# Two-layer hybrid attention encoder: DMA loads in a written order at the start of attention, and softmax reciprocals spread through DRAM

## The chip, the cores and the metric

One NeuronCore of a Trainium2 chip runs the whole kernel. The metric is the device time of one execution in microseconds (us); the time of a kernel is the median of its runs. TensorE multiplies matrices and transposes, VectorE, ScalarE and GpSimd work on elements, SyncE (SP) issues most of the DMA transfers. In the profile they are PE, DVE, ACT, POOL and SP; PEld is TensorE's loading of weights.

## The reference

A trunk of two layers on 1024 tokens of width 1024. Each layer normalises `x`, projects it once to 2656 columns, and runs three groups of attention heads side by side:

```python
def hybrid_layer(x, g_norm, w_in, ...):
    z = rms_norm(x, g_norm) @ w_in
    aq, ak, av, ag, bq, bk, bv, bg, cq, ckv, ckr, cg = split(z)
    # A: 6 heads of 64, 2 key heads, all 1024 keys
    oa = dense_gqa_blocks(rope(norm(aq)), rope(norm(ak)), av) * silu(ag)
    # B: 6 heads of 64, 2 key heads, keys within 128 positions, a sink logit per head
    ob = windowed_sink_gqa(rope(bq), rope(bk), bv, sink) * silu(bg)
    # C: 4 heads of 64 + 32 rotary, low-rank q and kv, all 1024 keys
    oc = mla_blocks(...) * silu(cg)
    return x + concat(oa, ob, oc) @ w_out
```

After the second layer a last RMSNorm follows. Every softmax divides by its row's sum: here the reciprocals of these sums are multiplied into the gate, and the gate into the output.

## The kernel before

Everything is float32 split into a high and a low part, so that a product of two matrices is two or three passes of TensorE (`mm3`, line 136). Per layer the stages are: norm and transposes of `x` with the value projection, the projections of groups A, B and C, the gate projection (`pg`), attention, and the output projection (`pw`). Queries, keys, values and gates go through DRAM tensors (`d_q`, `d_k`, `d_kn`, `d_vc`, `d_gate`), attention's outputs through `d_o`.

Attention is a list of units that `units` yields and `pipeline` works off. A unit is one head (A, C) or three heads (B) of one 128-query tile: scores on TensorE (`sa`, `sb`, `sc`), a maximum on VectorE (L684, L922), the exponential on ScalarE with its row sum (L694, L942), transposes of the probabilities on TensorE (`ppa`, `ppb`, `ppc`, L703), their split into `pth` and `ptl` by ScalarE, GpSimd and VectorE (L710 to L715), and products with the values (`poa`, `pob`, `poc`). `pipeline` puts the scores of one unit ahead of the transposes of the unit before, and pieces of older value products between them. The query tile `qt` runs from 0 to 7 with six units of A and two of B each; C's units (groups of three query tiles; two head pairs `hp` of 0 and 1) are strewn between them after the half tiles in `C_AT`, and what remains of C follows at the end. Within these priorities a scheduler places each engine's instructions, the DMA issues of SP included; an engine then works them off in order.

`Gqa(g, qt, m0)` is a query tile of A or B: it loads the queries by four DMAs (`qsta`, `qstb`, in `qstack`), and takes the output tile `o`; its `gate` loads the gate (`gta`, `gtb`). `KeysC` loads group C's keys (`k`, in six DMAs for the first pair) and its values (`vC`), `GroupC` its queries by five DMAs a tile (`qc`). At the start of attention come A's and B's keys and first queries, the sink and the mask, then C's keys and queries, then the gates, by the program's order.

`divided` (L749 to L767) turns sums into gate factors, once for each query tile of A and of B and once for each group of C: 22 times in a layer. A query's sum lies on its partition, and the gate has queries along its free axis, so the reciprocals have to be turned: VectorE takes them (`rc`, L755), GpSimd copies each to 64 columns (`rw`, 128x384, one buffer, L757), TensorE transposes the three 128x128 blocks (`pr`, L763), ScalarE copies them out (`rb`, L765), and GpSimd multiplies the gate by them (L767). Later GpSimd multiplies the output by the gate (L800, L1090), and SP stores it to `d_o`.

`dma` (L93) issues on SP; in attention all its DMAs stay behind the last load of weights (`queue_behind`). Names in the profile leave out buffer numbers.

Of the kernel before, what the change touches and what calls it, by code (L numbers as in the profile page):

```python
# [8 lines left out]
F32 = mybir.dt.float32  # L9
# [36 lines left out]
def kernel(  # L46
# [22 lines left out]
    P = 128  # L69
    S, D = x.shape[1], x.shape[2]  # L70
    DEPTH = norm_g.shape[0]
    NS = S // P
# [5 lines left out]
    small = ctx.enter_context(tc.tile_pool(name="small", bufs=4))  # L78
    dram = ctx.enter_context(tc.tile_pool(name="dram", bufs=1, space=DRAM))

    queue_behind = [None]
    last_pow = [None]

    def after(ins, first):

        tc.add_manual_dep(
            ins,
            first.name,
            mybir.DependencyInfo(mybir.DependencyClass.NoSync, mybir.DependencyReason.DATA),
            reason="order",  # L90
        )
        return ins

    def dma(dst, src, eng=None):

        a, b = (t.bitcast(F32) if t.dtype == F32R else t for t in (dst, src))
        ins = (eng or nc.sync).dma_start(a, b)  # L97
        if queue_behind[0] is not None and eng is None:
            after(ins.ins, queue_behind[0])
        return ins.ins  # L100

    pinned = [False]
# [13 lines left out]
    V, G, A, T = Engine(nc.vector), Engine(nc.gpsimd), Engine(nc.scalar), Engine(nc.tensor)  # L116

    ident = const.tile([P, P], F32, name="ident")
    dma(ident, c_ident)
    mhalf = const.tile([P, 8], F32, name="mhalf")  # L120
    nc.vector.memset(mhalf, -0.5)
# [104 lines left out]
    for l in range(DEPTH):  # L226
# [8 lines left out]
        d_kn = dram.tile([2, 2, P, S], F32R, name=f"d_kn{l}")  # L235
        d_k3 = dram.tile([2, 64, S], F32R, name=f"d_k3{l}")
        d_vc = dram.tile([P, NS, 4, P], F32R, name=f"d_vc{l}")
        d_o = dram.tile([P, 8, S], F32, name=f"d_o{l}")

        vp_ = ExitStack()  # L240
# [4 lines left out]
        with stage.ph as ph:  # L245
# [6 lines left out]
            def ps_t(name):  # L252
                return ps1.tile([P, 512], F32, tag="T", name=name)
# [24 lines left out]
            if l == 0:  # L278
# [6 lines left out]
                def load_x(st):  # L285
                    xts[st] = stage.px.tile([P, D], F32, tag="xt", name=f"xt{l}_{st}", bufs=XBUFS)
                    queue_behind[0] = dma(xts[st], x_src[st * P : (st + 1) * P, :])
# [61 lines left out]
            for i in range(2):  # L349
                gq = g_small[:, i * 64 : i * 64 + 64]  # L350
                ins = G.tensor_tensor(
                    out=tabs[:, :, 2 * i, :],
                    in0=rope_a[:, :, 0, :],
                    in1=gq.unsqueeze(1).to_broadcast([P, NS, 64]),
                    op=ALU.mult,
                )
                after(ins.ins, behind)
                gv = gq.rearrange("p (h a c) -> p h a c", h=2, a=2)
                for a in range(2):
                    for h in range(2):  # L360
                        o = h * 32 + a * 16
                        ins = G.tensor_tensor(
                            out=tabs[:, :, 2 * i + 1, o : o + 16],
                            in0=rope_a[:, :, 1, o : o + 16],
                            in1=gv[:, h, 1 - a, :].unsqueeze(1).to_broadcast([P, NS, 16]),
                            op=ALU.mult,
                        )
# [22 lines left out]
            for st in range(NS):  # L390
                nm = f"{l}_{st}"
# [42 lines left out]
            for st in range(NS):  # L434
                nm = f"{l}_{st}"
# [219 lines left out]
        with ExitStack() as ph:  # L655
            ps2 = wa_.enter_context(tc.tile_pool(name=f"ps2_{l}", bufs=2, space=PSUM, reuse_waits="tile"))
            at = ph.enter_context(tc.tile_pool(name=f"at{l}", bufs=2, reuse_waits="tile"))
# [4 lines left out]
            pk_ = ExitStack()  # L662
            pk = pk_.enter_context(tc.tile_pool(name=f"pk{l}", bufs=1, side="right", reuse_waits="tile"))
            pq = pk_.enter_context(tc.tile_pool(name=f"pq{l}", bufs=1, side="right", reuse_waits="tile"))
            tcnt, qcnt = [0], [0]

            def ps_s(name):
                return ps2.tile([P, 512], F32, tag="S", name=name, bufs=SBANKS)
# [79 lines left out]
                    dma(t[r0 : r0 + 64, :, par, :], d_q[g][qt, i, 64 * par : 64 * par + 64])  # L748
                return t  # L749

            def divided(gt, sums, n, nm):

                pr = ps_t(f"pr{nm}")
                rc = small.tile([P, 3, 2], F32, tag="rc", name=f"rc{nm}")
                V.reciprocal(rc[:, 0:n, :], sums)  # L755
                wide = at.tile([P, 384], F32, tag="rw", name=f"rw{nm}", bufs=1)
                G.tensor_copy(  # L757
                    wide[:, 0 : n * P].rearrange("p (m a d) -> p m a d", a=2, d=64),
                    rc[:, 0:n, :].unsqueeze(3).to_broadcast([P, n, 2, 64]),
                )  # L760
                for m in range(n):
                    ms = slice(m * P, (m + 1) * P)
                    T.transpose(pr[:, ms], wide[:, ms], ident)  # L763
                rb = at.tile([P, 384], F32, tag="rb", name=f"rb{nm}")
                A.copy(rb[:, 0 : n * P], pr[:, 0 : n * P])  # L765
                gv = gt.rearrange("p g s -> p (g s)") if len(gt.shape) == 3 else gt
                G.tensor_tensor(out=gv, in0=gv, in1=rb[:, 0 : n * P], op=ALU.mult)  # L767

            class Gqa:
# [25 lines left out]
                def divide(self):  # L795

                    divided(self.gt, self.sm.rearrange("p (m a) -> p m a", a=2), 3, self.nm)

                def finish(self):
                    G.tensor_tensor(out=self.o, in0=self.o, in1=self.gt, op=ALU.mult)  # L800
                    dma(d_o[:, self.m0 : self.m0 + 3, self.qt * P : (self.qt + 1) * P], self.o)

            def pipeline(units, spare):


# [45 lines left out]


            if True:
                ks, start = {}, {}
                for g, m0 in (("a", 0), ("b", 3)):
                    start[g] = Gqa(g, 0, m0)
# [200 lines left out]
            class GroupC:  # L1057
# [25 lines left out]
                    dma(self.gt[:, 0 : self.n], d_gate[:, 6 + self.hp, self.q0 * P : self.q1 * P])  # L1083

                def divide(self):
                    divided(self.gt[:, 0 : self.n], self.sm.rearrange("p a g -> p g a"), self.nq, self.nm)

                def finish(self):
                    gt, o = self.gt[:, 0 : self.n], self.o[:, 0 : self.n]
# [39 lines left out]
            def groups_c():  # L1129
                for hp in range(2):  # L1130
                    ks = KeysC(hp)
                    for q0 in range(0, NS, 3):
                        c = GroupC(ks, hp, q0)
                        if hp or q0:
                            c.gate()
                        else:

                            for it in (start["a"], start["b"], c):
                                it.gate()
                            yield None  # L1140
                        for par in range(2):
                            grp = {}
                            yield [UnitC(c, par, g, grp) for g in range(c.nq)]

            def units():

                cs = groups_c()
                next(cs)
                for qt in range(NS):
                    if qt == 0:  # L1150
                        a, b = start["a"], start["b"]
                    else:
                        a, b = Gqa("a", qt, 0), Gqa("b", qt, 3)
                        a.gate()
                        b.gate()
                    for kv in range(2):
                        grp = {}
                        for g in range(3):
                            yield UnitA(a, kv, g, grp)
                            if g == 1:  # L1160
                                yield UnitB(b, kv)
                        if 2 * qt + kv in C_AT:
                            yield from next(cs)
                first = True
                for us in cs:
                    for u in us:
                        yield u
                        if first:
                            yield ab_done
                            first = False  # L1170
# [8 lines left out]
        with ExitStack() as ph:  # L1179
# [10 lines left out]
            for st in range(NS):  # L1190
                nm = f"{l}_{st}"
# [111 lines left out]
```

## Time and profile before

| | before |
|---|---|
| median of 3 runs (lowest to highest) | 1340.75 us (1340.05 to 1341.09) |
| the profiled execution's own time | 1342.18 us |
| its span in the profile | 1340.4 us |
| mean granted clock of TensorE | 0.988 of full speed |
| TensorE busy | 1301.9 us, 97% |
| VectorE busy | 892.3 us, 67% |
| ScalarE busy | 720.2 us, 54% |
| GpSimd busy | 524.6 us, 39% |

The profile is one execution. Busy times are unions of an engine's instructions; matmuls are pipelined, so TensorE's busy time says that it had something in flight, not that it ran at its peak. Attention's first scores start at 278.7 us in layer 0 and at 937 in layer 1; its last value products start at 598 and 1258. The number in the brackets of a timeline's row is the idle time of the engine before that instruction and what ended it.

### The profile page before, as it was taken

What the parts mean: (1) busy time and instruction counts of PE and PEld (TensorE: products, weight loads), DVE (VectorE), ACT (ScalarE), POOL (GpSimd) and SP (SyncE); (2) the same over time, 40 slices, a digit from 0 to 9 for tenths busy, and PEclk for the clock granted to TensorE, in tenths of its full rate; (3) what the DMA queues carried; (4) which work ended last, traced back from release to release, by engine and by line L of the source; (5) the groups of instructions that cost most, each with busy time, mean ns of one, the idle gap of its engine ahead of it and who ended that gap; (6) DMA issues with size and microseconds to landing.
All of it is one profiled execution on the core that took longest, in us unless ns stands there. A gap on an engine that the chain in (4) does not pass through costs nothing.

```text
span 1340.4 us, 21695 instructions
## 1 busy us (share of the span) xinstructions
PE 1301.9 (97%) x7320; PEld 1139.5 (85%) x7320; DVE 892.3 (67%) x2246; ACT 720.2 (54%) x1547; POOL 524.6 (39%) x602
## 2 busy tenths in 40 slices
PE   7999999989999999999999999999799999999997
PEld 7888998868989899888898889887698999998786
DVE  6685662057888988875537766600789899998543
ACT  4232341166888889842313324311688899897332
POOL 4330121025666676752023111300366766667100
PEclk8999999998999999999999999999899999999999
DMA  7234469353222432257323344783622225113443
GB/s 252 87 124 148 135 202 261 122 132 89 68 61 60 111 90 58 74 179 235 131 78 121 122 132 161 242 196 103 154 68 64 59 69 139 46 45 126 165 146 112
DMA packets 176878, 166.46 MB, mean 124 GB/s; under 512 B 22528, under 2 KB 149376, under 8 KB 176768
## 3 DMA queue, kind: packets, MB, share of 16 engines
q1 hardware_dynamic: 158016, 140.43, 36.5%
q10 hardware_dynamic: 18752, 24.65, 5.3%
q8 instruction: 58, 0.95, 0.3%
q14 instruction: 52, 0.43, 0.1%
HBM read 107.35 MB, written 57.67 MB: 123 GB/s over the span
## 4 chain that ended last, share of the span: by engine, by line
PE 82%; DVE 6%; DMA 5%; ACT 2%; issue 2%; SPq 2%; POOL 1%; POOLq 0%; DVEq 0%; ACTq 0%
PE pg L136 13%; PE pw L136 12%; PE pzb L114 7%; PE pza L114 7%; PE poa L136 6%; PE sc L136 5%; PE ppa L703 4%; PE pzc L136 4%; PE sa L136 4%; PE pzv L136 4%; PE ppc L703 3%; PE poc L136 3%; PE pob L136 2%; PE sb L136 2%; SPq L97 2%
## 5 line engine op out<-in xcount | busy, mean ns | idle before, releaser
L684 DVE CUSTOM_DVE_ANT_0 pa<-sa,zero 128x512 f32<-128x512 f32 x96 | 65.5, 682 | 136.6 <-PE sa L136 134.8
L711 POOL TENSOR_SCALAR ptha<-pfa 128x512 fp32r<-128x512 f32 x96 | 59.4, 621 | 206.7 <-ACT pfa L710 202.3
L712 POOL TENSOR_TENSOR ptla<-pfa,ptha 128x512 fp32r<-128x512 f32 x96 | 123.6, 1290 | 6.1
L136 PE MATMUL sa<-ka,qsta 128*128 128x512 f32 x384 | 121.3, 417 | 0.8 <-ACT g L617 0.7
L694 ACT ACTIVATE pa<-pa,nmxa 128x1024 f32<-128x1024 f32 x96 | 111.2, 1160 | 14.0 <-DVE nmxa L684 13.9
L136 PE MATMUL sc<-k,qc 128*128 128x512 f32 x384 | 111.5, 410 | 0.9 <-DVE nmxc L684 0.9
L703 PE MATMUL ppa<-ident,pa 128*128 128x128 f32 x768 | 106.3, 273 | 0.7 <-DVE ptlb L715 0.5
L703 PEld LDWEIGHTS ppa<-ident,pa 128*128 128x128 f32 x768 | 90.9, 141 | 14.8 <-DVE ptla L715 1.2
L136 PE MATMUL pw<-woh,oh 128*128 128x512 f32 x256 | 99.4, 394 | 2.1 <-ACT oh L1001 1.1
L136 PE MATMUL pw<-wol,oh 128*128 128x512 f32 x256 | 100.6, 394 | 0.8 <-DVE wol L1021 0.6
L136 PE MATMUL pg<-hTh,wh 128*128 128x512 f32 x256 | 100.3, 392 | 0.0
L136 PE MATMUL pg<-hTh,wl 128*128 128x512 f32 x256 | 100.2, 391 | 0.0
L136 PE MATMUL pg<-hTl,wh 128*128 128x512 f32 x256 | 100.1, 391 | 0.0
L136 PE MATMUL pw<-woh,ol 128*128 128x512 f32 x256 | 99.1, 393 | 0.3 <-DVE ol L1002 0.3
L216 POOL TENSOR_SCALAR wh<-wst 128x512 fp32r<-128x512 f32 (+1 forms) x64 | 39.6, 638 | 148.3 <-PE pzb L114 79.4
L617 ACT ACTIVATE g<-pg 128x512 f32<-128x512 f32 x32 | 19.1, 598 | 137.5 <-PE pg L136 90.5
L136 PE MATMUL poa<-ptha,vAB 128*128 128x384 f32 x256 | 89.4, 349 | 1.0 <-DVE ob L793 1.0
L136 PE MATMUL poa<-ptla,vAB 128*128 128x384 f32 x256 | 88.2, 344 | 0.0
L694 ACT ACTIVATE pc<-pc,nmxc 128x1024 f32<-128x1024 f32 x64 | 74.0, 1157 | 10.2 <-DVE nmxc L684 9.7
L136 PEld LDWEIGHTS sc<-k,qc 128*128 128x128 f32 x384 | 66.6, 189 | 10.7 <-DVE nmxc L684 2.0
L712 POOL TENSOR_TENSOR ptlc<-pfc,pthc 128x512 fp32r<-128x512 f32 x56 | 74.0, 1327 | 1.5
L684 DVE CUSTOM_DVE_ANT_0 pa<-sa,zero,nmxa 128x512 f32<-128x512 f32 x96 | 71.1, 743 | 4.5 <-PE sa L136 1.8
(217 smaller groups left out, 3817.3 us busy)
## 6 DMA issues: line engine op xcount, KB each, us to landing
wst<-in_w_in_dram SPq DMA_DIRECT2D x20, 512.0 KB, 3.6
d_gate<-g ACTq DMA_DIRECT2D x32, 256.0 KB, 2.4
wost<-in_w_out_dram SPq DMA_DIRECT2D x32, 256.0 KB, 2.9
wst<-in_w_in_dram SPq DMA_DIRECT2D x16, 384.0 KB, 4.4
qsta<-d_qa SPq DMA_DIRECT2D x64, 96.0 KB, 2.6
qstb<-d_qb SPq DMA_DIRECT2D x64, 96.0 KB, 2.6
k<-d_kn SPq DMA_DIRECT2D x12, 512.0 KB, 6.8
qc<-d_qc SPq DMA_DIRECT2D x96, 64.0 KB, 2.2
```

Source lines behind the costliest of these rows:

```text
L97: ins = (eng or nc.sync).dma_start(a, b)
L114: return lambda *a, **k: tc.keep_in_program_order(f(*a, **k))
L136: T.matmul(ps, lhsT=a, rhs=b, start=first and i == 0, stop=last and i == len(parts) - 1)
L216: G.tensor_scalar(h, f, 1.0, 0.0, ALU.mult, ALU.add)
L617: A.activation(g, ps, AF.Silu)
L684: V.tensor_tensor_reduce(p[:, c * 512 : (c + 1) * 512], ps, zero[:, 0:1].to_broadcast([P, 512]), -1.0, nmx[0][:, 0:1] if c else 3.0e38, AL ...
L694: A.activation(p, p, AF.Exp, scale=-1.0, bias=nmx[1][:, 0:1], accum_out=sm)
L703: T.transpose(pt[:, (j - q0) * P : (j - q0 + 1) * P], p[:, j * P : (j + 1) * P], ident)
L711: G.tensor_scalar(hi, f, 1.0, 0.0, ALU.mult, ALU.add)
L712: G.tensor_tensor(out=lo, in0=f, in1=hi.bitcast(F32), op=ALU.subtract)
```

## The change

It has three parts. `divided` gets a second way, used for all groups but the last two of C's second head pair (`near`): the reciprocals are transposed as they are (128x6 to 6x128, L776), ScalarE copies the six rows (`rt`, L778), SP stores them to a DRAM tensor `d_r`, and two DMAs load them back into `rb`, each spreading three rows over 64 partitions. `in_order` makes the DMAs of SP keep the program's order from the start of attention until the first group of C is made. And `units` makes the objects of query tile `qt + 1` (their query loads) in the middle of tile `qt`, and the gates of the first tile of A and B ahead of C's keys.

```diff
         if queue_behind[0] is not None and eng is None:
             after(ins.ins, queue_behind[0])
+        if in_order[0] and eng is None:
+            tc.keep_in_program_order(ins)
...
+        d_r = dram.tile([4 * NS, 6, P], F32, name=f"d_r{l}")
...
-            def divided(gt, sums, n, nm):
+            def divided(gt, sums, n, nm, near=False):
...
+                if near:
...
+                else:
+                    rc = rc.rearrange("p a m -> p (a m)")[:, 0 : 2 * n]
+                    V.reciprocal(rc.rearrange("p (a m) -> p m a", a=2), sums)
+                    T.transpose(pr[0 : 2 * n, 0:P], rc, ident)
+                    rt = at.tile([16, P], F32, tag="rt", name=f"rt{nm}")
+                    A.copy(rt[0 : 2 * n, :], pr[0 : 2 * n, 0:P])
+                    dr = d_r[rcnt[0], 0 : 2 * n]
+                    rcnt[0] += 1
+                    dma(dr, rt[0 : 2 * n, :])
+                    drv = dr.rearrange("(a m) s -> a (m s)", a=2)
+                    for a in range(2):
+                        dma(rb[64 * a : 64 * a + 64, 0 : n * P], drv[a].partition_broadcast(64))
                 gv = gt.rearrange("p g s -> p (g s)") if len(gt.shape) == 3 else gt
                 G.tensor_tensor(out=gv, in0=gv, in1=rb[:, 0 : n * P], op=ALU.mult)
...
             if True:
+                in_order[0] = True
...
-                    divided(self.gt[:, 0 : self.n], self.sm.rearrange("p a g -> p g a"), self.nq, self.nm)
+                    divided(self.gt[:, 0 : self.n], self.sm.rearrange("p a g -> p g a"), self.nq, self.nm, self.hp and self.q0)
...
-                            for it in (start["a"], start["b"], c):
-                                it.gate()
+                            c.gate()
                             yield None
...
+                a, b = start["a"], start["b"]
+                ahead = Gqa("a", 1, 0), Gqa("b", 1, 3)
+                a.gate()
+                b.gate()
                 cs = groups_c()
                 next(cs)
+                in_order[0] = False
                 for qt in range(NS):
-                    if qt == 0:
-                        a, b = start["a"], start["b"]
-                    else:
-                        a, b = Gqa("a", qt, 0), Gqa("b", qt, 3)
+                    if qt:
+                        a, b = ahead
                         a.gate()
                         b.gate()
                     for kv in range(2):
+                        if kv and 0 < qt < NS - 1:
+                            ahead = Gqa("a", qt + 1, 0), Gqa("b", qt + 1, 3)
```

How it moves instructions. SP at the start of attention in layer 0, before (`qstb_1` are the queries of B's second tile, `k_0` parts of C's keys, `qc_0_0` C's first queries):

```order
L97 DMA vC_0_2815<-d_vc_85 128x8x256
L97 DMA gta_0_2844<-d_gate_77 128x3x128
L97 DMA gtb_0_2846<-d_gate_77 128x3x128
L97 DMA gtc_0_0_2848<-d_gate_77 128x384
L97 DMA qsta_1_3133<-d_qa_78 64x3x128 x4
L97 DMA qstb_1_3140<-d_qb_79 64x3x128
L97 DMA k_0_0_2814<-d_kn_83 64x2x1024 x2
...
L97 DMA qc_0_0_2824<-d_qc_80 64x2x128 x2
...
L97 DMA qstb_1_3140<-d_qb_79 64x3x128 x3
L97 DMA gta_1_3147<-d_gate_77 128x3x128
```

and with the change:

```order
L98 DMA qsta_1_2815<-d_qa_78 64x3x128 x4
L98 DMA qstb_1_2822<-d_qb_79 64x3x128 x4
L98 DMA gta_0_2829<-d_gate_77 128x3x128
L98 DMA gtb_0_2831<-d_gate_77 128x3x128
L98 DMA k_0_0_2833<-d_kn_83 64x2x1024 x2
...
L98 DMA vC_0_2834<-d_vc_85 128x8x256
L98 DMA qc_0_0_2843<-d_qc_80 64x2x128 x2
...
L98 DMA gtc_0_0_2863<-d_gate_77 128x384
L98 DMA gta_1_3148<-d_gate_77 128x3x128
```

The four `qstb_1` stand together ahead of the keys; the two gates and `vC_0` now stand ahead of `qc_0_0`.

TensorE at the same place, before (`sb_1`: scores of B's second tile; `sa_1`: A's; `prb`: B's divisor transposes; `poa`: value products):

```order
L136 MATMUL sb_1_0_0_3240<-kb_0_2802,qstb_1_3140 128x384
L703 MATMUL ppb_0_1_2_0_3117<-ident,scb_0_1_3038 128x128 x2
L136 MATMUL sb_1_0_1_3244<-kb_0_2802,qstb_1_3140 128x384
L136 MATMUL sb_1_0_2_3248<-kb_0_2802,qstb_1_3140 128x384
L136 MATMUL sa_1_0_2_0_3287<-ka_0_2789,qsta_1_3133 128x512
L763 MATMUL prb_0_3122<-ident,rwb_0_3125 128x128 x3
L136 MATMUL poa_0_0_2_3025<-ptha_0_0_0_0_2874,vAB_90 128x384
```

and with the change (`sc_0_0_0`: the first scores of C):

```order
L139 MATMUL sb_1_0_2_3249<-kb_0_2803,qstb_1_2822 128x384
L139 MATMUL sa_1_0_2_0_3288<-ka_0_2790,qsta_1_2815 128x512
L139 MATMUL sa_1_0_2_1_3292<-ka_0_2790,qsta_1_2815 128x512
L707 MATMUL ppb_0_1_1_0_3121<-ident,scb_0_1_3053 128x128 x2
L139 MATMUL sc_0_0_0_0_0_3332<-k_0_0_2833,qc_0_0_2843 128x512
L139 MATMUL poa_0_0_2_3040<-ptha_0_0_0_0_2889,vAB_91 128x384
```

The first `sc` has moved ahead of the sixteen `poa`.

GpSimd at the divisions of the third query tile, before:

```order
L757 COPY rwb_2_4108<-rcb_2_4106 128x384
L757 COPY rwa_2_4176<-rca_2_4174 128x384
L767 TENSOR_TENSOR gtb_2_3762<-gtb_2_3762,rbb_2_4113 128x384
L711 TENSOR_SCALAR ptha_2_1_0_1_3993<-pfa_2_1_2_4_4167 128x4x128
L767 TENSOR_TENSOR gta_2_3760<-gta_2_3760,rba_2_4181 128x384
L712 TENSOR_TENSOR ptla_2_1_0_1_3995<-pfa_2_1_2_4_4167,ptha_2_1_0_1_3993 128x4x128
```

and with the change:

```order
L715 TENSOR_SCALAR ptha_2_1_0_1_4008<-pfa_2_1_2_4_4182 128x4x128
L716 TENSOR_TENSOR ptla_2_1_0_1_4010<-pfa_2_1_2_4_4182,ptha_2_1_0_1_4008 128x4x128
L786 TENSOR_TENSOR gtb_2_3763<-gtb_2_3763,rbb_2_4121 128x384
L715 TENSOR_SCALAR pthc_0_3_0_0_1_4222<-pfc_0_3_0_0_4_4240 128x4x128
L716 TENSOR_TENSOR ptlc_0_3_0_0_1_4224<-pfc_0_3_0_0_4_4240,pthc_0_3_0_0_1_4222 128x4x128
L786 TENSOR_TENSOR gta_2_3761<-gta_2_3761,rba_2_4189 128x384
```

The copies `rw` are gone, and both multiplications stand behind one split (`pth`, `ptl`) more.

SP with the change at the first divisions, where the new DMAs stand among query loads and output stores:

```order
L98 DMA qc_0_3_4131<-d_qc_80 64x2x128
L98 DMA d_r_86<-rtb_0_3142 6x128
L98 DMA d_r_86<-rta_0_3196 6x128
L98 DMA rbb_0_3138<-d_r_86 64x384 x2
L98 DMA rba_0_3192<-d_r_86 64x384 x2
L98 DMA d_o_87<-ob_0_2802 128x3x128
L98 DMA gta_2_3761<-d_gate_77 128x3x128
```

The stores to `d_r` and the loads of `rb` stand in front of the first store to `d_o` and of the gates of the third tile.

## Rows read from the trace of the kernel before

**Rows 1.** The page's part 1 (busy us, share, instructions) and part 4 (the chain).
```profile
PE 1301.9 (97%) x7320; PEld 1139.5 (85%) x7320; DVE 892.3 (67%) x2246; ACT 720.2 (54%) x1547; POOL 524.6 (39%) x602
...
PE 82%; DVE 6%; DMA 5%; ACT 2%; issue 2%; SPq 2%; POOL 1%; POOLq 0%; DVEq 0%; ACTq 0%
```

**Rows 2.** Stretches: length, busy PE, PEld, DVE, ACT, POOL; clock, DMA share, GB/s.
```profile
278.00:282.00 4.00, 3.75 (x16) 2.37 (x14) 2.69 (x9) 2.48 (x3) 0.00 (x0) 1.00 0.59 170
282.00:286.00 4.00, 3.91 (x26) 3.46 (x27) 3.57 (x17) 3.81 (x11) 0.79 (x2) 1.00 0.73 177
286.00:290.00 4.00, 3.83 (x22) 2.66 (x21) 3.86 (x15) 4.00 (x11) 2.25 (x3) 1.00 1.02 213
...
302.00:306.00 4.00, 2.31 (x7) 1.88 (x8) 1.52 (x5) 0.00 (x0) 0.00 (x0) 0.50 0.66 188
...
340.00:560.00 220.00, 217.29 (x1379) 196.87 (x1378) 193.01 (x534) 190.27 (x410) 149.45 (x167) 1.00 0.26 69
```

**Rows 3.** TensorE's timeline, layer 0: start, length, instruction, idle before and its releaser.
```profile
296.50 0.44 PE L703 MATMUL ppb<-ident,scb 128*128 128x128 f32 x2 [0.35 <-ACT pfa L710]
303.45 0.98 PE L136 MATMUL sb<-kb,qstb 128*128 128x384 f32 x2 [6.50 <-DMA qstb<-d_qb]
...
305.09 1.62 PE L136 MATMUL sb<-kb,qstb 128*128 128x384 f32 x4 [0.24 <-DMA qstb<-d_qb]
```

**Rows 4.** TensorE's timeline at the same place of layer 1.
```profile
960.64 0.98 PE L136 MATMUL sb<-kb,qstb 128*128 128x384 f32 x2 [5.62 <-DMA qstb<-d_qb]
...
962.51 1.65 PE L136 MATMUL sb<-kb,qstb 128*128 128x384 f32 x4 [0.46 <-DMA qstb<-d_qb]
```

**Rows 5.** SP's timeline at the start of attention, layer 0.
```profile
277.48 2.48 SPq L97 DMA_DIRECT2D qsta<-d_qa  x4
280.02 0.65 SPq L97 DMA_DIRECT2D qstb<-d_qb  x1
281.90 2.19 SPq L97 DMA_DIRECT2D k<-d_kn  x3
284.15 1.87 SPq L97 DMA_DIRECT2D k<-d_k  x3
286.06 14.86 SPq L97 DMA_DIRECT2D qc<-d_qc  x15
300.97 1.82 SPq L97 DMA_DIRECT2D qstb<-d_qb  x3
```

**Rows 6.** The chain that ended last, in order of time: start, length, what.
```profile
285.42 10.77 DMA k<-d_k
...
302.19 2.77 DMA qstb<-d_qb
...
313.99 0.33 PE pra L763 x3
```

**Rows 7.** Groups by line and form: busy us, mean ns of one, idle before, releasers.
```profile
L763 PE MATMUL pra<-ident,rwa 128*128 128x128 f32 x48 | 9.6, 272 | 0.0
...
L757 POOL COPY rwa<-rca 128x384 f32<-128x384 f32 x16 | 8.1, 505 | 56.2 <-PE prb L763 35.1 <-DVE nmxa L684 12.5 <-issue 5.9
...
L765 ACT COPY rba<-pra 128x384 f32<-128x384 f32 x16 | 7.9, 491 | 0.4 <-PE pra L763 0.4
...
L939 ACT ACTIVATE besb<-besb 128x3 f32<-128x3 f32 x32 | 6.2, 193 | 0.0
```

**Rows 8.** DMA issues: size of one, median us from issue to landing.
```profile
qsta<-d_qa SPq DMA_DIRECT2D x64, 96.0 KB, 2.6
...
vC<-d_vc SPq DMA_DIRECT2D x4, 1024.0 KB, 6.7
...
gta<-d_gate SPq DMA_DIRECT2D x16, 192.0 KB, 2.8
...
d_o<-ob SPq DMA_DIRECT2D x16, 192.0 KB, 2.1
```

**Rows 9.** Waits of SP over the whole run: total us, times, longest.
```profile
SPq L97 <- POOL ob L800: 134.0, 16, 19.0
```

More of the change, by code (lines that the diff above doesn't have):

```diff
@@ L81 @@
     queue_behind = [None]
+    in_order = [False]
     last_pow = [None]
@@ L664 @@
             pq = pk_.enter_context(tc.tile_pool(name=f"pq{l}", bufs=1, side="right", reuse_waits="tile"))
-            tcnt, qcnt = [0], [0]
+            tcnt, qcnt, rcnt = [0], [0], [0]
             def ps_s(name):
@@ L749, in qstack @@
                 return t
-            def divided(gt, sums, n, nm):
+            def divided(gt, sums, n, nm, near=False):
                 pr = ps_t(f"pr{nm}")
[L754 to L763, printed above, removed]
-                rb = at.tile([P, 384], F32, tag="rb", name=f"rb{nm}")
-                A.copy(rb[:, 0 : n * P], pr[:, 0 : n * P])
+                rb = at.tile([P, 384], F32, tag="rb", name=f"rb{nm}")
+                rc = small.tile([P, 2, 3], F32, tag="rc", name=f"rc{nm}")
+                if near:
+                    rc = rc.rearrange("p a m -> p (a m)").rearrange("p (m a) -> p m a", a=2)[:, 0:n, :]
+                    V.reciprocal(rc, sums)
+                    wide = at.tile([P, 384], F32, tag="rw", name=f"rw{nm}", bufs=1)
+                    G.tensor_copy(
+                        wide[:, 0 : n * P].rearrange("p (m a d) -> p m a d", a=2, d=64),
+                        rc.unsqueeze(3).to_broadcast([P, n, 2, 64]),
+                    )
+                    for m in range(n):
+                        ms = slice(m * P, (m + 1) * P)
+                        T.transpose(pr[:, ms], wide[:, ms], ident)
+                    A.copy(rb[:, 0 : n * P], pr[:, 0 : n * P])
+                else:
[10 more added lines that the diff above has]
+                        dma(rb[64 * a : 64 * a + 64, 0 : n * P], drv[a].partition_broadcast(64))
```

## The prediction

> **What bounds the kernel now.** I began with the page's table of busy time and its chain of waits: TensorE is busy 97% of the span, and 82% of the chain that ended last lies on it, against 6% on VectorE and 5% on transfers [rows 1]. Then I cut the span into stretches. In the steady part of layer 0's attention, 340 to 560 us, TensorE is busy 217.29 of 220 us at a granted clock of 1.00, VectorE 193.01, ScalarE 190.27, GpSimd 149.45 [rows 2]. So there a microsecond taken off TensorE should mostly be a microsecond off the time, while GpSimd has a third of its time free.
>
> The other place is the start of attention. TensorE's timeline shows it idle for 6.50 us, from 296.94 to 303.45, before the first scores of group B's second query tile (`sb`), and 0.24 us more before the next pair; the releaser is the load of `qstb` [rows 3]. Layer 1 shows the same, 5.62 and 0.46 us [rows 4]. [...] SP's timeline tells why the load is late: one of the tile's four pieces is issued at 280.02, then six loads of `k` and fifteen of `qc`, which take SP to 300.97, and only then the other three [rows 5]. The chain agrees: a `k` load, then SP's issues, then `qstb<-d_qb` 2.77 us [rows 6]. At 286 to 290 us the DMA engines are full, share 1.02 at 213 GB/s [rows 2].
>
> **Part 1: the transposes.** Forty of the 44 divisions (20 of 22 in each layer) replace their three transposes by one of 6x128 (the two-tile groups: two by one of 4x128). That removes 40 x 3 - 2 = 118 and adds 40: 78 fewer. One transpose lasts 272 ns [rows 7], but they are pipelined: three in a row take 0.33 us on the chain [rows 6], 0.11 us each. 78 x 0.11 = **8.5 us**. The bounds are 0 (TensorE would have waited for something else) and 78 x 0.272 = 21 us; I take the pipelined price because the steady stretch has few gaps to fill.
>
> **Part 2: copies.** GpSimd loses 40 wide copies of 0.505 us, ScalarE's copy of 128x384 at 491 ns becomes one of 6x128, nearest to the small activation of 193 ns [rows 7]: 20 us off GpSimd, 40 x 0.3 = 12 us off ScalarE. I cost both at **nothing**: TensorE's work covers them. If that cover were gone in part they would be a gain, 3 us at most by ScalarE's share of the chain (2% [rows 1], 12 of its 720 us); I keep that inside the range.
>
> **Part 3: the detour through DRAM.** Each of these divisions now goes reciprocal, transpose, ScalarE copy, a 3 KB store to `d_r`, two broadcast loads of 96 KB into `rb`, GpSimd's multiplication. The nearest transfers are `d_o<-ob` at 2.1 us and `qsta` at 2.6 us [rows 8], and SP spends about 0.6 us on an issue (2.48 us for four [rows 5]): 2.1 + 2.6 + 2 x 0.6 = 5.9 us, against 0.505 + 0.33 + 0.491 = 1.3 us for copy, transposes and copy before. So `rb` comes an estimated 4.6 us later. It is wanted by the multiplication of the gate, then by that of the output, then by the store; none feeds TensorE before the output projection. But two queues are held. SP waits in place for the ScalarE copy and for the store's landing, with query loads, gates and `d_o` stores behind it; SP already sits 134.0 us waiting for `ob` products [rows 9], and the query loads are issued one query tile ahead, so I take their delay as covered. GpSimd waits in place for `rb`, with the splits of the transposed probabilities (`pth`, `ptl`) behind it, which TensorE's value products need. The order puts the multiplication some instructions later than the old copy, behind a split or two, which hides most of the 5.9 us. I take **+2.5 us** for all of this; the bounds are 0 and 40 x 4.6 = 184 us, were each late `rb` to reach TensorE in full; 2.5 is close to the lower end because GpSimd is busy only 149.45 of 220 us [rows 2]. Also inside it: the next layer's norm weights are now loaded behind the first output rows, which is near its use.
>
> [...]
>
> **Part 4: the start of attention.** The four `qstb_1` loads now stand together, ahead of `k`, so that wait goes [rows 3, 4]. What it cost: 6.50 + 0.24 us idle, and the half-rate stretch from 303.45 to about 308, half of 4.6, 2.3 us: 9.0 us in layer 0, some 8 in layer 1. What is late next: the first scores of group C (`sc`), which TensorE's order now puts ahead of the 16 value products of `poa` and which need `k` and `qc_0_0`. In front of `qc_0_0` the pinned queue has newly put `vC_0` (1024 KB), two gates (2 x 192 KB) and three pieces of `qstb` (3 x 96 KB) [rows 8]: 1696 KB, or 1.74 MB. At 213 GB/s that is 8.2 us; before the full stretch the engines have idle share 0.41 and 0.27 in the two windows from 278 to 286 [rows 2], 4 x 0.68 = 2.7 us, which takes up part of it. So `qc_0_0` lands about 5.5 us later than now. Now it is no earlier than the `k` piece in front of it, which is done at 285.42 + 10.77 = 296.2 [rows 6]: about 302. TensorE, with no wait for `qstb`, runs 2.5 to 3 us of scores and transposes past 296.94 and stands at `sc` by about 299.7. That is a new stall of 2.5 to 4.5 us and some 1.5 us of lower clock: 5 us in place of 9. I take **4 us per layer, 8 in all**; the bounds are 0 (the whole wait only changes its name) and 17 (no stall is left). Moving `vC_0` itself costs nothing where it is used, some 35 us later.
>
> Making the next query tile's objects half a tile earlier moves only loads that are early already: **0**.
>
> **Sum.** -8.5 + 0 + 2.5 - 8 = -14.0 us against the profiled execution's 1342.18 us: 1328.2. The median of the runs, 1340.75, lies 1.43 below that execution, so **1327 us** on the scale of the medians.
>
> **The rivals.** Two of the changes in 1000 are about what a measurement of this kernel can tell from none: 2.7 us.
> - *GpSimd becomes the bound (slower).* Each late `rb` stops GpSimd, the splits behind it come late, and TensorE waits for them in `poa`, `poc`, `pob`. For it: the splits are in-order work on the same engine. Against it: GpSimd's third of free time, and the multiplication's later place. Parts 1 and 4 give 16.5 us; with 2.7 us on top, it takes 19.2 / 40 = 0.48 us per division reaching TensorE before the time is slower. At 0.7 us: 1340.75 - 16.5 + 28 = 1352. Chance 0.09.
> - *The start's wait only changes its name.* `vC_0` and the gates push `qc_0_0` to 305 or later, and TensorE idles as long as before at `sc`. For it: the full DMA engines. Part 4 is then 0: 1335. Chance 0.16.
> - *No new stall at the start.* `qc_0_0` lands by 300, or the scheduler's other work covers it; part 4 is 17: about 1317 to 1318. Chance 0.14.
> - *The transposes were hidden.* TensorE isn't what limits the steady stretch; VectorE and ScalarE are busy 88% and 86% of it [rows 2], so their chain may be, and part 1 gives nothing: about 1335. Chance 0.12. [...]
> - *Both gains fail*, or the losses of part 3 eat them: within 2.7 us of now. Chance 0.10.
>
> **How the numbers follow.** The forecast has the remaining 0.39. The range takes in the second to fourth rivals and the unknown 0 to 10 us of part 3: 1315 to 1338, which leaves out the rival that is slower and most of the last, 0.2 at most. Faster: 0.39 + 0.16 + 0.14 + 0.12 = 0.81; same 0.10; slower 0.09.
>
> **What would show it.** Right: 78 fewer transposes for `pr`; no idle time at `sb` for `qstb`; a gap of some 3 us before the first `sc`, released by a `qc` or `k` load; the steady stretches of both layers some 4 us shorter each, with TensorE's busy share unchanged; GpSimd's multiplication released now and then by a load of `rb`, with no matching idle time on TensorE. Wrong: idle time on TensorE at `poa` or `poc` released by `pth` or `ptl` of GpSimd; a gap at `sc` as long as the old one; a steady stretch that keeps its length though the transposes are gone; query loads that come late because SP stood at `d_r`.

## The result, and the profile after

The changed kernel takes **1383.78 us** (median of 4 runs, 1383.21 to 1384.62) against 1340.42 for the kernel before: a ratio of 1.0323, 95% interval 1.0305 to 1.0341. It is 3.2% slower. 1327 was forecast, in a range of 1315 to 1338; the chance given to "slower" was 0.09.

The page of the kernel after, its parts 1 and 4, to set against [rows 1]:

```profile
PE 1304.0 (94%) x7242; PEld 1130.2 (82%) x7242; DVE 886.5 (64%) x2246; ACT 711.6 (51%) x1547; POOL 504.9 (37%) x562
...
PE 71%; DMA 11%; DVE 6%; ACT 4%; issue 3%; POOL 3%; SPq 2%; POOLq 0%; DVEq 0%; ACTq 0%
```

78 transposes are gone (7320 to 7242 matmuls), yet TensorE's busy time has not shrunk, its share of the chain has fallen from 82 to 71%, and that of transfers has risen from 5 to 11%. So the kernel waits for transfers where it did not before. TensorE's timeline at the start of attention says where, layer 0 and then layer 1 (start, length, instruction, idle time before it and its releaser):

```profile
282.15 2.78 PE L139 MATMUL sa<-ka,qsta 128*128 128x512 f32 x5 [4.02 <-DMA ka<-d_ka]
292.16 0.98 PE L139 MATMUL sb<-kb,qstb 128*128 128x256 f32 x3 [7.22 <-DMA kb<-d_kb]
...
320.17 1.62 PE L139 MATMUL sc<-k,qc 128*128 128x512 f32 x3 [6.67 <-DMA qc<-d_qc]
...
967.47 2.55 PE L139 MATMUL sa<-ka,qsta 128*128 128x512 f32 x5 [3.03 <-DMA ka<-d_ka]
...
977.60 0.98 PE L139 MATMUL sb<-kb,qstb 128*128 128x256 f32 x3 [7.58 <-DMA kb<-d_kb]
...
1005.33 1.62 PE L139 MATMUL sc<-k,qc 128*128 128x512 f32 x3 [6.69 <-DMA qc<-d_qc]
```

The wait for `qstb_1` of [rows 3, 4] is gone, as forecast. In its place stand three, 17.9 us of idle time in layer 0 and 17.3 in layer 1. The third, at `sc`, was forecast (2.5 to 4.5 us) and is longer, 6.67 and 6.69; the other two are for loads that the prediction did not look at: the keys of A and B (`ka`, `kb`), which in the kernel before were there long ahead. SP's timeline shows their issue, first before, then after:

```profile
208.51 3.76 SPq L97 DMA_DIRECT2D qsta<-d_qa  x4
212.48 2.54 SPq L97 DMA_DIRECT2D ka<-d_ka  x4
215.06 2.67 SPq L97 DMA_DIRECT2D qstb<-d_qb  x4
219.73 6.16 SPq L97 DMA_DIRECT2D kb<-d_kb  x4
```

```profile
206.70 0.34 SPq L98 DMA_DIRECT2D d_qc<-qklc  x1
236.66 22.21 SPq L98 DMA_DIRECT2D qsta<-d_qa  x4
263.84 12.08 SPq L98 DMA_DIRECT2D ka<-d_ka  x4
275.96 8.62 SPq L98 DMA_DIRECT2D qstb<-d_qb  x4
284.68 2.56 SPq L98 DMA_DIRECT2D kb<-d_kb  x4
...
299.79 1.89 SPq L98 DMA_DIRECT2D k<-d_kn  x3
...
304.47 19.36 SPq L98 DMA_DIRECT2D qc<-d_qc  x15
```

The same sixteen loads in the same order, but they begin 28 us later, are spread over 50 us, and push everything behind them: `k` is issued at 299.79 (281.90 before [rows 5]). What SP waits for is in the list of waits (total us, times, longest), before and after:

```profile
SPq L97 <- DMA d_gate<-g: 68.9, 8, 14.6
```

```profile
SPq L98 <- DMA d_gate<-g: 140.3, 16, 29.6
```

The wait has doubled. In layer 0, eight of the waits now end at loads of `qsta`, `ka` and `qstb`, which read no gate. The windows show what that does to the bandwidth: in the gate projection's stretch the kernel after moves 126 GB/s (180 before), and soon behind it the engines are full (columns as in [rows 2]):

```profile
186.00:279.00 93.00, 92.13 (x418) 76.02 (x416) 15.16 (x38) 16.64 (x29) 7.42 (x13) 1.00 0.39 126
279.00:292.00 13.00, 2.78 (x5) 1.33 (x5) 2.74 (x8) 3.13 (x5) 0.00 (x0) 0.60 0.80 183
292.00:306.00 14.00, 11.64 (x63) 9.51 (x63) 9.11 (x33) 7.64 (x20) 3.96 (x5) 0.88 1.07 220
...
340.00:560.00 220.00, 210.49 (x1302) 186.10 (x1301) 186.63 (x515) 180.59 (x393) 142.14 (x151) 0.99 0.31 87
```

The granted clock falls with the waits: 0.60 and 0.88 in the second and third row. In the trace TensorE's granted clock is 0.50 from 281.6 to 295.3 and from 315.8 to 326.0 us, 23.9 us in this start; in the kernel before it is 10.2 us (298.3 to 308.6).

The last of these rows answers to the steady stretch of [rows 2]: TensorE is busy 210.49 us of 220 there, not 217.29, so a second, smaller loss lies in the steady part.

**A wait that no order of instructions shows.** In the traces each DMA of SP or ScalarE bears the number of a semaphore that its landing raises. There are eight of these numbers, 106 DMAs on each before (848 in all) and 121 after (968), in turn over both queues; they are the counters that the experiments speak of. In the kernel before, 840 DMAs have another ahead of them on their semaphore, eight places back, and not one of the 840 is issued until that one has landed. The eight loads of layer 0 that wait for a gate store with the change, and the store eight places back (start of the issue, us):

| load, on SP | issued | gate store, on ScalarE | apart |
|---|---|---|---|
| `qsta` | 236.66 | 234.59 | 2.07 |
| `qsta` | 242.06 | 240.03 | 2.03 |
| `qsta` | 252.92 | 250.91 | 2.01 |
| `qsta` | 258.36 | 256.35 | 2.01 |
| `ka` | 263.84 | 261.79 | 2.05 |
| `ka` | 269.28 | 267.23 | 2.05 |
| `ka` | 274.69 | 272.67 | 2.02 |
| `qstb` | 282.76 | 278.12 | 4.64 |

SP's own order is the same at this place. In the sequence over both queues, though, the first `qsta` was DMA 154 (counted from 0) and is now 166: twelve more of ScalarE's gate stores have come ahead of it, 15 in place of 3. From 212.83 us on ScalarE issues one of these stores every 5.44 us, each behind a `g` that has waited 4.84 us for TensorE to finish a piece of the gate projection. The loads had been issued under that projection, from 208.51 us on; now they trickle behind its stores.

### The profile page after: what moved, and what is told of

The parts are those of the page before. It is cut to its first block, busy times and chain, and to the rows that moved or that the text cites. A ratio compares the mean times of both kernels' runs of the same rounds, so it can differ in the third digit from the quotient of the medians.

```text
span 1382.8 us, 21728 instructions
## 1 busy us (share of the span) xinstructions
PE 1304.0 (94%) x7242; PEld 1130.2 (82%) x7242; DVE 886.5 (64%) x2246; ACT 711.6 (51%) x1547; POOL 504.9 (37%) x562
## 4 chain that ended last, share of the span: by engine, by line
PE 71%; DMA 11%; DVE 6%; ACT 4%; issue 3%; POOL 3%; SPq 2%; POOLq 0%; DVEq 0%; ACTq 0%
PE pg L139 12%; PE pw L139 10%; PE pzb L117 6%; PE pza L117 6%; PE poa L139 5%; PE pzc L139 4%; PE sc L139 4%; PE ppa L707 4%; PE pzv L139 3%; PE sa L139 3%; PE poc L139 2%; SPq L98 2%; PE ppc L707 2%; DMA qc<-d_qc 2%; DMA kb<-d_kb 1%
## 5 line engine op out<-in xcount | busy, mean ns | idle before, releaser
L139 PE MATMUL sa<-ka,qsta 128*128 128x512 f32 x384 | 126.3, 427 | 11.1 <-DMA ka<-d_ka 7.0
L698 ACT ACTIVATE pa<-pa,nmxa 128x1024 f32<-128x1024 f32 x96 | 110.9, 1156 | 23.3 <-DVE nmxa L688 23.1
L139 PEld LDWEIGHTS sa<-ka,qsta 128*128 128x128 f32 x384 | 63.9, 193 | 24.8 <-issue 7.9
L719 DVE TENSOR_TENSOR ptla<-ppa,ptha 128x512 fp32r<-128x512 f32 x96 | 64.9, 682 | 25.3 <-ACT ptha L718 25.2
```

What stands on the lines that cost most here:

```text
L139: T.matmul(ps, lhsT=a, rhs=b, start=first and i == 0, stop=last and i == len(parts) - 1)
L698: A.activation(p, p, AF.Exp, scale=-1.0, bias=nmx[1][:, 0:1], accum_out=sm)
L719: V.tensor_sub(lo, ptv, hi.bitcast(F32))
```

## The experiments

Two theories stood at first. P: the pin of the written order is to blame, by these semaphores. D: the detour through DRAM is to blame.

**Order alone**: every division the old way.

```diff
-            def divided(gt, sums, n, nm, near=False):
+            def divided(gt, sums, n, nm, near=True):
...
-                    divided(self.gt[:, 0 : self.n], self.sm.rearrange("p a g -> p g a"), self.nq, self.nm, self.hp and self.q0)
+                    divided(self.gt[:, 0 : self.n], self.sm.rearrange("p a g -> p g a"), self.nq, self.nm)
```

> The written order and the earlier query objects alone; every division goes the old way (three transposes). Theory P (the pin is to blame: it puts the first loads of attention behind the gate stores in the program's own sequence of DMAs, and a DMA issued on any queue waits for the completion of an earlier one of that sequence): the start keeps its stalls at sa, sb and sc, some 14 us of idle time a layer more than before plus the slower clock after them, so 1367 to 1378 us. Theory D (the detour through DRAM is to blame, the start costs little): 1335 to 1348 us.

1375.07 us, ratio 1.0257 (1.0235 to 1.0279). P holds; the idle times at `sa`, `sb` and `sc` are 3.79, 7.73 and 6.57 us in layer 0. From the end of the gate projection to the last `poa` of layer 0, the kernel before and then this run (columns as in [rows 2]):

```profile
278.82:562.50 283.68, 273.32 (x1707) 245.58 (x1707) 243.67 (x677) 239.52 (x518) 182.12 (x203) 0.98 0.30 80
```

```profile
277.05:577.33 300.28, 276.96 (x1707) 247.10 (x1707) 239.71 (x677) 239.16 (x518) 181.99 (x203) 0.97 0.37 92
```

The stretch is 16.6 us longer: TensorE's idle time in it is 23.3 us in place of 10.4, and the other 3.6 us are busy time for as many matmuls, with 20.5 us at a granted clock of 0.50 in place of 10.2. Layer 1 is 14.6 us longer there. The two make up most of the run's 34 us.

**Divide alone**: the new `divided` in the kernel before.

> The new division alone, with the loads ordered by the scheduler as before. Theory P: the start is as before; in the steady part the 78 transposes fewer (8.5 us) stand against some 12 us of idle time that the late rb makes, so 1336 to 1350 us. Theory D: 1365 us or more.

1354.02 us, ratio 1.0100 (1.0085 to 1.0115): 13 us slower, just above what P allowed and far under D. It is not the order of the kernel before, though: the scheduler placed the loads at the start anew, `qc` now partly ahead of `k` and of `qsta`, and the wait there stands at `sa`, as long as the one at `sb` was:

```profile
298.94 3.75 PE L136 MATMUL sa<-ka,qsta 128*128 128x512 f32 x8 [6.37 <-DMA qsta<-d_qa]
```

From the first `sc` to the last `poa` TensorE idles 8.05 and 8.46 us in the two layers (2.71 and 2.15 in the kernel before). In this order of loads the new division costs more than it saves; how much of the 13 us is the detour's and how much the other order's is not told apart.

**The pin later, and no pin**, the rest of the change kept:

```diff
-                in_order[0] = True
                 ks, start = {}, {}
...
+                in_order[0] = True
                 a, b = start["a"], start["b"]
```

> The changed kernel, but the pin begins only after the loads of A's and B's keys, first queries, sink and mask. Theory P: these loads are issued during the gate projection again (qsta near 208 us, not 236), the idle times at sa and sb go (11.3 us in layer 0, 10.6 in layer 1, and the slow clock after them), what is left of the loss is the stall at sc and the detour: 1345 to 1358 us. Theory D: within 5 us of the changed kernel's 1384.

> The changed kernel without any pin; new division and earlier query objects stay. Theory P: like the run with the later pin, 1340 to 1358 us, whichever order the scheduler gives the loads of C. Theory D: within 5 us of 1384.

1338.03 us, ratio 0.9979 (0.9965 to 0.9994), and 1337.13 us, 0.9979 (0.9965 to 0.9992). Both fall by 46 to 47 us to a little under the kernel before, and below the ranges that were expected, so what P left to the stall at `sc` and the detour was too much. SP's and TensorE's timelines of the run without a pin:

```profile
208.69 3.30 SPq L98 DMA_DIRECT2D qsta<-d_qa  x4
212.03 2.56 SPq L98 DMA_DIRECT2D ka<-d_ka  x4
```

```profile
303.75 0.93 PE L139 MATMUL sc<-k,qc 128*128 128x512 f32 x3 [3.98 <-DMA qc<-d_qc]
...
320.40 0.44 PE L139 MATMUL poa<-ptla,vAB 128*128 128x384 f32 x1 [1.90 <-POOL ptla L716]
```

The loads are back at 208 us, and the only long wait at the start is the one at `sc`, 3.98 us (2.64 in layer 1), which the prediction had put at 2.5 to 4.5. The 1.90 us at `poa`, released by GpSimd's `ptla`, are the sign that it had named for its first rival. The pin in itself brings nothing here: SP's order at the start is the same without it.

**The shared counters by themselves**: the pin stays, the gate stores move from ScalarE's queue to GpSimd's. The author took it that they then share no semaphore with SP's loads.

```diff
-                            dma(d_gate[:, m0 + m, hf * 512 : (hf + 1) * 512], g, nc.scalar)
+                            dma(d_gate[:, m0 + m, hf * 512 : (hf + 1) * 512], g, nc.gpsimd)
```

> [...] If the shared counters are the cause, the loads run during the gate projection again though the pin stays, the idle times at sa and sb go, and the time falls from 1384 to 1335 to 1348 us, near the run with the later pin (1338). Rival: the pin holds the loads by itself, whatever the counters (SP's queue waits for something else); then it stays above 1370 us.

1350.80 us, ratio 1.0077 (1.0055 to 1.0099): 33 us of the loss go although the pin and SP's order stay. Its timeline:

```profile
205.64 3.15 SPq L98 DMA_DIRECT2D qsta<-d_qa  x4
208.83 2.57 SPq L98 DMA_DIRECT2D ka<-d_ka  x4
```

So it is the gate stores on ScalarE's queue that held the loads, as the shared semaphores have it, and the rival (the pin holds them by itself) falls. Which semaphores GpSimd's stores raise is not shown; issued there, they do not hold SP's loads. The time stays 3 us above the range that was expected; the rest lies in layer 0 behind the start. From the first `sc` to the last `poa` this run takes 267.5 us in layer 0 and 257.1 in layer 1, the run without a pin 254.9 and 257.3, the changed kernel 266.9 and 257.2 (taken from these instructions' first start and last end). Of the 12.6 us between this run and the one without a pin in layer 0, 7.5 are idle time of TensorE (11.37 and 3.89 us).

**Where the steady part loses.** The changed kernel and the last run have that place in common. The chain of waits of the changed kernel there, in order of time:

```profile
469.45 0.26 ACT rtb L778
469.73 5.79 DMA d_r<-rtb
475.54 3.23 DMA rbb<-d_r
...
479.07 0.09 POOL gtb L786
...
480.76 1.27 POOL ptla L716
482.06 0.59 ACT pfc L714
...
482.69 0.84 PE ppa L707 x4
```

and the idle times of GpSimd and TensorE that it makes:

```profile
479.07 1.02 POOL L786 TENSOR_TENSOR gtb<-gtb,rbb 128x384 f32<-128x384 f32 x1 [12.30 <-DMA rbb<-d_r]
```

```profile
482.69 0.84 PE L707 MATMUL ppa<-ident,pa 128*128 128x128 f32 x4 [2.19 <-ACT pfc L714]
```

This is the first rival of the prediction, step by step: the 3 KB store takes 5.79 us to land, with three loads of `k` of 512 KB each issued in the 5 us before it; `rb` is late; GpSimd stands 12.30 us; the split `ptla` behind it is late; ScalarE's next copy waits 3.62 us for that split; TensorE idles. But the store is not alone in it. The first load of `rbb` has the semaphore of the third of these `k` loads (issued at 466.35), eight places back. SP's waits between 470 and 478 us:

```profile
SPq L98 <- DMA k<-d_kn: 3.3, 2, 2.2
SPq L98 <- DMA d_r<-rtb: 0.8, 1, 0.8
```

SP waits 2.2 us for `k` in front of `rbb`, to 474.65, and only then 0.8 us more for the store, to 475.52: had the store landed sooner, `rbb` could have been issued 0.8 us sooner, no more. Over the run GpSimd waits 42.2 us for `rbb`:

```profile
POOL gtb L786 <- DMA rbb<-d_r: 42.2, 11, 12.3
```

The place is one of several: in the run with the gate stores on GpSimd the same chain at the first divisions is longer, 7.66 us of GpSimd and then 3.50 us of TensorE at 322.56.

**The earlier query objects alone**: no pin, old division.

> The earlier query objects alone: no pin, and every division the old way. Against the run without a pin (1337 us, new division) it gives the net worth of the new division once the start is in order. If the transposes are worth their 8.5 us and the detour is free: about 1346 us. If the detour gives back what the transposes save: 1335 to 1339. If the detour costs more than that: under 1335.

1337.38 us, ratio 0.9975 (0.9959 to 0.9990), the same as with the new division. Without the pin the new division's net worth is nothing that can be measured.

**What a transpose is worth.** Two runs on the kernel before, one with 84 transposes left out (the factors of the other heads are left out with them), one with 128 added:

```diff
-                for m in range(n):
-                    ms = slice(m * P, (m + 1) * P)
-                    T.transpose(pr[:, ms], wide[:, ms], ident)
+                T.transpose(pr[:, 0:P], wide[:, 0:P], ident)
...
+                    pr[:, 0:P].unsqueeze(1).to_broadcast([P, n, P]),
```

> The kernel before, with one transpose in each division and its result used for all heads (so the factors of the other heads are left out): 84 transposes fewer, no detour, nothing else moved. If TensorE's time is what counts in the steady part: 84 x 0.11 = 9.2 us less, 1330 to 1333 us. If the transposes were hidden (the chain through VectorE and ScalarE sets the pace): 1338 to 1342.

1349.23 us, ratio 1.0068 (1.0044 to 1.0092): a miss by both expectations, slower. The scheduler placed other work differently; a row of TensorE's timeline shows where some of it went, a wait in the output projection that the kernel before does not have:

```profile
626.34 0.80 PE L136 MATMUL pw<-woh,oh 128*128 128x512 f32 x1 [6.57 <-ACT oh L1002]
```

From the gate projection's end to the last `poa` it takes 283.2 and 283.4 us, the kernel before 283.7 and 285.5: 2.6 us less, in the stretch that 78 of the 84 have left. The run doesn't price a transpose cleanly.

> The kernel before with each of the divisions' transposes done twice: 128 more on TensorE, nothing else added. If TensorE sets the pace of the steady part, 128 x 0.11 = 14 us more: 1352 to 1357. If such transposes lie in time that TensorE has anyway: 1338 to 1346.

1351.55 us, ratio 1.0069 (1.0051 to 1.0088), just under the first expectation. Of 1341.59 us that is 9.3 us for 128, 0.07 us each (0.05 to 0.09 by the interval), against the 0.11 that was taken. In the traces, from the end of the gate projection to the end of the output projection, TensorE is busy 13.1 us more, 0.10 each, and idle 2.1 us less.

**C's values behind its first queries**: the run without a pin, with the `vC` load and the first gates moved behind `qc`.

```diff
-                    dma(self.v, d_vc[:, :, 2 * hp : 2 * hp + 2, :])
+                    if hp:
+                        self.values()
...
                         else:
+                            ks.values()
                             c.gate()
...
+                cs = groups_c()
+                next(cs)
                 a.gate()
                 b.gate()
-                cs = groups_c()
-                next(cs)
```

> The kernel without the pin, with C's values (vC) and the first gates loaded behind C's first queries. If what is left at the start is the wait for qc behind 1.4 MB of other loads, the idle time at sc (4.0 us in layer 0, 2.6 in layer 1) and the slower clock behind it go: 1327 to 1333 us. Rival: another load is late instead (k itself, or vC at the first value products of C): 1335 to 1340.

1328.46 us, ratio 0.9918 (0.9894 to 0.9941), as expected: the wait at `sc` is gone. In the window from 279 to 310 us, first of the kernel before and then of this run, TensorE's busy time rises from 23.35 to 29.58 us and its granted clock from 0.83 to 1.00:

```profile
279.00:310.00 31.00, 23.35 (x121) 18.45 (x120) 24.22 (x75) 21.97 (x50) 11.48 (x13) 0.83 0.71 170
```

```profile
279.00:310.00 31.00, 29.58 (x174) 24.34 (x175) 27.97 (x91) 28.69 (x70) 11.41 (x12) 1.00 0.84 202
```

**The same order with the old division; with the store on ScalarE's queue; with the old division at four places a layer.**

> The fastest order so far (no pin, C's values behind its first queries) with the old division throughout. If the new division's net worth is nothing, as without the pin: within 3 us of 1328. If its transposes count once the start is in order: 1332 to 1338. If the detour costs more than it saves: 1318 to 1325.

1328.97 us, ratio 0.9899 (0.9885 to 0.9914): again the same as with the new division. The two traces differ all the same. From the end of the gate projection to the end of the output projection, both layers of one execution added up (length, busy times), the new division and then the old:

```profile
sum 786.12, PE 766.05 PEld 665.49 DVE 615.77 ACT 556.07 POOL 405.70; mean PE 383.02 PEld 332.75 DVE 307.89 ACT 278.04 POOL 202.85
```

```profile
sum 787.09, PE 774.24 PEld 675.13 DVE 617.92 ACT 566.28 POOL 427.17; mean PE 387.12 PEld 337.57 DVE 308.96 ACT 283.14 POOL 213.58
```

With the new division TensorE is busy 8.2 us less and idle 7.2 us more (20.1 in place of 12.9). In the two runs without a pin, with the values in front, it is 4.4 less and 6.5 more, with 10 us more at a granted clock of 0.50. So the transposes' saving is there as busy time, and idle time takes its place.

```diff
-                    dma(dr, rt[0 : 2 * n, :])
+                    dma(dr, rt[0 : 2 * n, :], nc.scalar)
```

> The same order with the new division, but the store to d_r is issued by ScalarE, which has just made rt, so that SP no longer waits for rt; the loads of rb stay on SP. If the late rb comes of the store's place in SP's queue, GpSimd's waits for rb shrink (18.9 us at gtb in the run with C's values behind) and the time falls by 1 to 4 us below 1328. If it comes of the two transfers' own landing times or of the loads' place, it stays within 2 us, or rises by ScalarE's issues (40 x 0.6 us, partly hidden).

1339.34 us, ratio 0.9982 (0.9969 to 0.9994): 9 us worse by the ratios. GpSimd's wait for `rbb` did not shrink (20.8 us, 18.9 before), so the store's place in SP's queue was not what made it late. Part of the cost is a wait of the same kind. In each layer a copy on ScalarE that reads no gate starts only when a load of `gtb` has landed; that ScalarE's first store, in front of it, has the semaphore of that load, eight places back, is the author's reading:

```profile
307.35 0.48 ACT L740 COPY oha<-poa 64x384 f32<-64x384 f32 x1 [5.10 <-DMA gtb<-d_gate]
```

In layer 1 it is 3.37 us. TensorE idles 4.17 and 2.44 us behind these places (2.56 and 2.33 at others in the run with the store on SP), and in layer 0 its granted clock is 0.51 from 307 to 314 us (1.00 in the other run). What makes up the rest of the 9 us is not shown.

```diff
-divided(self.gt, self.sm.rearrange("p (m a) -> p m a", a=2), 3, self.nm)
+divided(self.gt, self.sm.rearrange("p (m a) -> p m a", a=2), 3, self.nm, self.qt in (0, 4))
```

> The order with C's values behind its first queries, where the run with the new division and the one with the old took the same time (1328 and 1329 us). Here the old division serves A and B of query tiles 0 and 4 alone, where the trace of that run shows GpSimd waiting 7.2 and 4.0 us for rb (behind the loads of C's queries and values, and of C's second keys); the other 32 stay new. If the late rb at these places is what eats the transposes' saving, the idle times of 2.6 and 2.3 us on TensorE near 315 and 968 us go, 16 transposes come back (1.2 us): 1321 to 1326. If the saving is lost elsewhere or was never there: 1327 to 1331.

1328.85 us, ratio 0.9920 (0.9903 to 0.9937): the theory missed. TensorE's idle times at 315 and 968 us are indeed gone, but between 340 and 615 us its idle time, summed over gaps above 0.05 us, is 7.1 us where it was 4.6, and behind 1010 us 6.7 where it was 4.1. So the saving does not go at these two places; which waits take it stays open.

## Why the prediction was wrong

**Part 4 failed, and with it the sign.** The step was "the four `qstb_1` loads now stand together, ahead of `k`, so that wait goes", followed by a sum that began at 278 us. It took as given that every load in front of them stays where it was, because its place in SP's queue stays. The place did; the wait did not. The pin moved the sixteen first loads behind twelve more gate stores in the sequence over both queues in which the eight semaphores are taken (the first `qsta` from 154 to 166). The runs price it: with and without the pin 1383.78 and 1337.13 us, 47 us with the new division; 1375.07 and 1337.38, 38 us, with the old. None of the five rivals held this mechanism. The chance of 0.09 stood on another one.

**What was right in part 4** shows as soon as the pin is gone: no wait for `qstb_1`, a new one at `sc` of 3.98 and 2.64 us (2.5 to 4.5 forecast), released by `qc`. The gain of all this with the old division is 1 - 0.9975, 3.4 us, in place of 8: the term was sized too high by more than half. The wait at `sc` is not what is missing: it came as forecast, and without it the time falls by another 8 us (new division) or 10 (old), where the term had 9 for it (17 less 8). But with that wait gone the whole gain is 13.5 us with the old division (11.5 to 15.4 by the interval), and not the 17 of the upper bound. So the removal of the old wait was priced some 3.5 us too high; why is not shown.

**Part 1** took 0.11 us a transpose and 8.5 us in all. As busy time this was nearly right: added transposes cost 0.10 us each, and with C's values behind the queries TensorE is busy 8.2 us less. As time it was not: 128 more cost 0.07 us each, and the 78 fewer bring nothing that can be measured, for idle time grows by about as much.

**Part 2** can't be told apart from the rest. ScalarE's small copy takes 0.26 us in the chain above, near the 0.193 taken.

**Part 3** was sized too low. Forecast were 2.5 us, to be set against the transposes' saving. Without the pin the time is the same with and without the detour, so it eats that saving; in the changed kernel it costs 8.7 us more than the saving (1383.78 less 1375.07), and in the run with the division alone, whose loads the scheduler also placed anew, up to 13 more. The two transfers were taken at 5.9 us with their issues. Where no large load stands just in front this is nearly right, as this chain of the changed kernel shows:

```profile
333.98 2.23 DMA d_r<-rtb
336.75 2.85 DMA rbb<-d_r
```

Behind loads of half a megabyte the store alone takes 5.79 us, and SP waits 2.2 us for one of them as well in front of the load of `rb`; the sum had no term for that. Nor does SP issue that load before the store has landed: `rbb` is issued at 475.54, and SP's wait for the store ends at 475.52.

**The rivals.** GpSimd as the bound did occur, but in a few places and for the smaller part of the loss. "The transposes were hidden" is neither shown nor excluded: added ones count, removed ones did not pay, but with the detour other waits came in their place, and the run that left them out without the detour was rearranged. "The start's wait only changes its name" described `sc`, with 4 us of idle time in the order that was meant (6.7 in the changed kernel), where the old wait was 6.7 and 6.1. That the best order's 1328 us lies next to the 1327 that were forecast is chance: it has no wait at `sc` and no gain from the transposes.

## What to carry to other kernels

In these traces SP's and ScalarE's DMAs are coupled through eight semaphores that they take in turn (in the kernel before, 840 of 840 were issued after the landing of the one eight places back): before trusting an order in one queue, look at what each DMA waits for, not only at what stands in front of it. It shows here in SP's loads behind gate stores (28 us) and in the load of `rb` behind `k` (2.2 us), and, as the author reads it, in ScalarE's copy behind a load of gates (5.10 us). The detour through DRAM cost two landings, 2.23 and 2.85 us in one place; behind large loads the small store alone took 5.79 us: a place where nothing large is in front, or a consumer that does not stand still for it, would be worth a try (neither was measured here). Here the whole gain (1328 us, 0.8 to 1.0% under the kernel before) comes from the order of a few loads at the start, without a pin.

## What had not been expected

A load of queries that needs nothing from the gate projection was issued 28 us later behind its stores (236.66 in place of 208.51), and shares nothing with them but a semaphore. A store of 3 KB took 2.23 us to land in one place and 5.79 in another. And 78 transposes on an engine that is busy 97% of the time could be removed without a gain in time, its idle time growing by what its busy time lost, while 128 more cost 9.3 us.
